# Two of four up pairs in three rounds of each MLP as units of seven products, with mixed norm operands

## The chip, the cores and the metric

The kernel runs on one core of one Trainium2 chip. The metric is the device time of one execution in microseconds, lower is better. The time before is the median of three runs, 1206.8 us (1206.55 to 1207.28 us).

## What is computed

The reference is one step of a two-layer decoder over 512 prompt tokens and 64 sample tokens that share all weights. Layer 0 mixes with retention and a gated MLP, layer 1 with sliding-window attention. Each layer ends with the part that this change touches:

```python
def sqrelu_mlp(h, w_up, w_down):
    return jnp.square(jax.nn.relu(h @ w_up)) @ w_down

hp = hp + sqrelu_mlp(rmsnorm(hp, norm_mlp[l]), mlp_w_up[l], mlp_w_down[l])
hs = hs + sqrelu_mlp(rmsnorm(hs, norm_mlp[l]), mlp_w_up[l], mlp_w_down[l])
```

The model width is 1024, the MLP width 4096, everything in float32. The 576 tokens are the columns of all activations: `h[0]` to `h[7]` hold 128 rows of the width each.

## The kernel before

TensorE (PE) multiplies in fp32r, and every operand is split into a high part and a low part. A product is three matmuls: high by high, high by low and low by high. ScalarE (ACT) casts the high part of a weight block (line 278), VectorE (DVE) subtracts it from the block to get the low part (line 289). The two parts of 128 x 512 weights are in six buffers each (`NW_`), filled ahead of use by `ahead_to`; the raw weights come by DMA, 512 KB each, into three buffers (`raw`, line 235) and a fourth one that shares its place with the tile `q` and serves every second unit of the down stage. A buffer is loaded again once `done` says that both halves of its weights are split.

An MLP runs four rounds. A round has an up stage and a down stage:

- The up stage takes eight chunks of 128 rows of the MLP's width. A chunk is 8 blocks of the width x 3 products x 2 halves of the tokens = 48 matmuls of 288 columns (line 334, `block`), with the norm's operands `xhi` and `xlo` as the moving side. DVE then applies the relu and the norm's factor to the PSUM tile `acc` (line 496), and ACT squares (line 501). Two chunks make a pair, whose four quarters are combined on DVE (`combine`, lines 533 to 536) into seven operands; these are split by ACT (`ahi`, line 504) and DVE (`alo`, line 505).
- The down stage takes four units. A unit makes a 2 x 2 block product out of seven products (the scheme of Strassen and Winograd) instead of eight: P1 to P7, each 4 blocks x 3 = 12 matmuls of 288 columns (line 346, `product`), so 84. Its weights are sums of raw blocks (s1 to s4, DVE, line 263), and its partial sums are passed on by copies in PSUM (`y`, `z`, `w`, ACT) and added to `h` by DVE (line 557). The first unit of a round runs four products over three of the four pairs first, and then over the fourth, so the last pair's operands are wanted some 36 matmuls after its start. The last unit of a round goes block by block, with the low weight part in its second matmul.

DVE and ACT keep the order in which the program is written (`manual_schedule`); PE is ordered by the scheduler. `norm.finish` (the factor `rstd`) comes after the first chunk of round 0. Below, pairs are numbered 0 to 3 and rounds 0 to 3 in each MLP.

Of the kernel before, what the change touches and what calls it, by code (L numbers as in the profile page):

```python
# [119 lines left out]
def hybrid_step(ctx: ExitStack, tc: tile.TileContext, a, o):  # L120
# [349 lines left out]
    def rounds_of(norm, nxt, mp):  # L470
        rounds, closing = 32 // FB, Closing(COL["fin"])

        def up():

            acc, got = acc_tile(), take(2)
            for k in range(KC):
                block([acc[:, hf, 0:TH] for hf in range(2)], cut(got, k), norm.xs[k], (0, 1), k == 0, k == KC - 1)
            ahead_to(used[0] + NW_ - 2)
            return acc[:, :, 0:TH]

        def flat(v):
            return v.rearrange("p a b -> p (a b)")

        for r in range(rounds):
            acts, firsts = [], []
            for p in range(FB // 2):

                q = mp.tile([P, 8, TH], F32, name="q", tag="q", bufs=1)
                hi = mp.tile([P, 7, TH], F32R, name="ahi", tag="ahi", bufs=FB // 2)
                lo = mp.tile([P, 7, TH], F32R, name="alo", tag="alo", bufs=FB // 2)  # L490
                for j in range(2):
                    view = up()
                    if r == 0 and p == 0 and j == 0:
                        norm.finish()
                    t = mp.tile([P, T], F32, name="t", tag="t")
                    nc.vector.scalar_tensor_tensor(out=halves(t), in0=view, scalar=0.0, in1=norm.rv,  # L496
                                                   op0=ALU.max, op1=ALU.mult)
# [2 lines left out]
                    seg = slice(2 * j, 2 * j + 2)  # L500
                    nc.scalar.activation(out=flat(q[:, seg]), in_=t, func=AF.Square)  # L501

                def two(s0, s1):
                    nc.scalar.copy(out=hi[:, s0 - 1:s1 - 1], in_=q[:, s0:s1])  # L504
                    nc.vector.tensor_tensor(out=lo[:, s0 - 1:s1 - 1], in0=q[:, s0:s1],  # L505
                                            in1=hi.bitcast(F32)[:, s0 - 1:s1 - 1], op=ALU.subtract)

                b12 = q[:, 0]
                combine(*(q[:, i] for i in range(8)))
                two(1, 4)  # L510
                two(4, 8)
                acts.append([[t_[:, i] for i in range(7)] for t_ in (hi, lo)])
                if nxt is None and r == rounds - 1:

                    bh, bl = (mp.tile([P, TH], F32R, name=n, tag=n, bufs=FB // 2) for n in ("b12h", "b12l"))
                    split_into(b12, bh, bl)
                    firsts.append((bh, bl))
# [884 lines left out]
def layouts(i):  # L1402
# [72 lines left out]
```

## Time and profile before

| | |
|---|---|
| runs, median of three | 1206.8 us |
| the profiled execution | 1204.73 us |
| its span, first to last instruction | 1202.9 us |
| mean granted TensorE clock | 0.997 |
| matmuls, instructions in all | 9130, 22619 |
| DMA, mean over the span | 91 GB/s, 109.43 MB |

The profile is one execution on the chip. PE is the matmuls, PEld the weight loads beside them. A row of instructions gives the start in us, the duration in us, the engine, the line, and what it writes and reads; in brackets stands how long the engine was idle before it and what ended that. The chain of waits follows from the last instruction back to what released each step. A row of the stretches view gives, for each engine, the busy time in the stretch and the instructions, then the granted clock, the DMA engines' busy share and GB/s.

### The profile page before, as it was taken

To read this page: it belongs to the slowest core of one execution; us is meant where nothing else is said; L and a number is where in the kernel's file an instruction comes from. 1 tells how busy PE (TensorE), PEld (TensorE's weight loads), DVE (VectorE), ACT (ScalarE), POOL (GpSimd) and SP (SyncE) were. 2 spreads that over 40 slices of the span, in tenths; PEclk is the share of its full clock that TensorE was granted. 3 is DMA by queue.
4 is the path that set the end of the run, shared out by engine and by line. 5 is a ranking of instruction groups with operands and counts; after the bars stand their busy time and mean duration, and the time that the engine had idled before them with its cause. 6 is when DMAs were issued, how large, how long until landed. Compare 5 with 4: busy or idle time off the path is not lost.

```text
span 1202.9 us, 22619 instructions
## 1 busy us (share of the span) xinstructions
PE 1182.9 (98%) x9130; PEld 1164.8 (97%) x9130; DVE 908.2 (76%) x1691; ACT 588.4 (49%) x1111; POOL 148.3 (12%) x130
## 2 busy tenths in 40 slices
PE   8999999999999999999999999999999999999996
PEld 8899999999999999999999998999999999999996
DVE  8977797987866876885797787546785795795696
ACT  6333554654534444443466877445453453453452
POOL 4444250000000000000002653220000000000000
PEclk9999999999999999999999999999999999999999
DMA  7343222322332232242223211122233233233322
GB/s 269 110 142 112 88 65 80 88 81 78 90 106 87 77 117 71 71 120 75 88 87 111 72 53 55 53 76 71 84 105 89 71 106 91 68 106 88 87 73 79
DMA packets 38264, 109.43 MB, mean 91 GB/s; under 512 B 4160, under 2 KB 12544, under 8 KB 38144
## 3 DMA queue, kind: packets, MB, share of 16 engines
q1 hardware_dynamic: 37440, 107.36, 29.1%
q8 instruction: 72, 1.18, 0.4%
q10 hardware_dynamic: 720, 0.62, 0.2%
q14 instruction: 32, 0.26, 0.1%
HBM read 102.92 MB, written 6.03 MB: 91 GB/s over the span
## 4 chain that ended last, share of the span: by engine, by line
PE 82%; DVE 10%; ACT 4%; DMA 3%; issue 1%; SPq 0%; DVEq 0%; ACTq 0%
PE acc L334 50%; PE acc L346 10%; PE y L346 4%; PE f L346 4%; PE w L346 3%; PE z L346 3%; DVE wlo L289 3%; DMA raw<-in_w_dn 2%; ACT s L1158 1%; DVE alo L505 1%; PE tpp L1218 1%; DVE h L557 1%; ACT ahi L504 1%; PE dn L334 1%; PE op L1233 1%
## 5 line engine op out<-in xcount | busy, mean ns | idle before, releaser
L334 PE MATMUL acc<-xhi,whi 128*128 128x288 f32 x1504 | 321.7, 295 | 0.3 <-DVE vz L809 0.3
L334 PE MATMUL acc<-xhi,wlo 128*128 128x288 f32 x1504 | 319.2, 293 | 0.0
L334 PE MATMUL acc<-xlo,whi 128*128 128x288 f32 x1504 | 318.6, 293 | 0.0
L289 DVE TENSOR_TENSOR wlo<-raw,whi 128x512 fp32r<-128x512 f32 x317 | 235.7, 757 | 68.8 <-ACT whi L278 67.5
L334 PEld LDWEIGHTS acc<-xhi,whi 128*128 128x128 f32 x1504 | 239.5, 188 | 1.6 <-issue 1.1
L334 PEld LDWEIGHTS acc<-xhi,wlo 128*128 128x128 f32 x1504 | 240.5, 188 | 0.3
L334 PEld LDWEIGHTS acc<-xlo,whi 128*128 128x128 f32 x1504 | 240.1, 188 | 0.0
L278 ACT CAST whi<-raw 128x512 fp32r<-128x512 f32 x317 | 188.9, 619 | 100.5 <-PE acc L334 73.3
L501 ACT ACTIVATE q<-t 128x576 f32<-128x576 f32 x64 | 44.0, 687 | 227.8 <-DVE t L496 227.8
L278 ACT CAST whi<-s 128x512 fp32r<-128x512 f32 x140 | 83.4, 621 | 72.4 <-DVE s L263 62.8
L496 DVE SCALAR_TENSOR_TENSOR t<-acc,rstd 128x576 f32<-128x576 f32 x64 | 48.3, 755 | 80.6 <-PE acc L334 80.4
L289 DVE TENSOR_TENSOR wlo<-s,whi 128x512 fp32r<-128x512 f32 x140 | 95.9, 697 | 10.8 <-ACT whi L278 10.8
L505 DVE TENSOR_TENSOR alo<-q,ahi 128x864 fp32r<-128x864 f32 x64 | 77.2, 1205 | 8.3 <-ACT ahi L504 8.3
L504 ACT CAST ahi<-q 128x864 fp32r<-128x864 f32 x64 | 66.6, 1041 | 13.5 <-DVE q L536 12.5
L346 PE MATMUL acc<-ahi,wlo 128*128 128x288 f32 x340 | 71.4, 298 | 0.6
L346 PE MATMUL acc<-ahi,whi 128*128 128x288 f32 x340 | 71.4, 295 | 0.0
L346 PE MATMUL acc<-alo,whi 128*128 128x288 f32 x340 | 70.4, 295 | 0.0
L1102 POOL TENSOR_TENSOR kl<-z,kh 64x512 fp32r<-64x512 f32 x4 | 5.5, 1374 | 475.1 <-ACT kh L1099 474.9
L263 DVE TENSOR_TENSOR s<-raw 128x512 f32<-128x512 f32 x70 | 48.7, 695 | 19.8 <-DMA raw<-in_w_dn 19.8
L346 PEld LDWEIGHTS acc<-ahi,wlo 128*128 128x128 f32 x340 | 53.5, 188 | 2.5 <-DVE wlo L289 2.5
L346 PEld LDWEIGHTS acc<-ahi,whi 128*128 128x128 f32 x340 | 54.0, 188 | 0.0
L346 PEld LDWEIGHTS acc<-alo,whi 128*128 128x128 f32 x340 | 53.7, 188 | 0.0
(386 smaller groups left out, 2118.8 us busy)
## 6 DMA issues: line engine op xcount, KB each, us to landing
raw<-in_w_up SPq DMA_DIRECT2D x64, 512.0 KB
raw<-in_w_dn SPq DMA_DIRECT2D x64, 512.0 KB
raw<-in_w_in SPq DMA_DIRECT2D x22, 512.0 KB
raw<-in_w_o SPq DMA_DIRECT2D x16, 512.0 KB
raw<-in_w_qkv SPq DMA_DIRECT2D x10, 512.0 KB
h<-in_xT SPq DMA_DIRECT2D x8, 288.0 KB
s<-in_s SPq DMA_DIRECT2D x4, 512.0 KB
out_ret_s<-s SPq DMA_DIRECT2D x4, 512.0 KB
```

The costliest lines, as they stand in the source:

```text
L263: nc.vector.tensor_tensor(out=sums[k, i], in0=x, in1=b[y], op=ALU.add)
L278: nc.scalar.copy(out=hi, in_=src)
L289: nc.vector.tensor_tensor(out=lo, in0=src, in1=hi.bitcast(F32), op=ALU.subtract)
L334: nc.tensor.matmul(out, lhsT=w_, rhs=x_[:, hf if isinstance(hf, slice) else half(hf)], start=(start and si == 0), stop=(stop and si == 2))
L346: nc.tensor.matmul(out, lhsT=w[wi][:, k * P:(k + 1) * P], rhs=x(k)[xi], start=(start and n == 0), stop=(stop and n == len(steps) - 1), ski ...
L496: nc.vector.scalar_tensor_tensor(out=halves(t), in0=view, scalar=0.0, in1=norm.rv, op0=ALU.max, op1=ALU.mult)
L501: nc.scalar.activation(out=flat(q[:, seg]), in_=t, func=AF.Square)
L504: nc.scalar.copy(out=hi[:, s0 - 1:s1 - 1], in_=q[:, s0:s1])
L505: nc.vector.tensor_tensor(out=lo[:, s0 - 1:s1 - 1], in0=q[:, s0:s1], in1=hi.bitcast(F32)[:, s0 - 1:s1 - 1], op=ALU.subtract)
L557: nc.vector.tensor_tensor(out=row[:, cols_], in0=row[:, cols_], in1=src, op=op)
L1158: nc.scalar.activation(out=s[:, n, cut_:], in_=s[:, n, cut_:], func=AF.Exp, bias=nm[:, n:n + 1], accum_out=den[:, n:n + 1])
L1218: nc.tensor.transpose(out=tp[:, i * P:(i + 1) * P], in_=s[:, n, hf * P:(hf + 1) * P], identity=ident)
```

## The change

In rounds 1 to 3 of each MLP, pairs 0 and 2 are no longer two chunks but one unit of seven products (`up_unit`). The activations are then the side with combinations: the norm's operands are mixed once per MLP in round 0 (`mix`, one for each two rows of `h`, after chunks 1, 2, 4 and 5), into sixteen tiles `xn`, eight of them new in the MLP's pool and eight in the place of `ks`. The weights of the unit are the same sums s1 to s4 as in a down unit, so the up weights are laid out by pairs in memory and a chunk takes the blocks of its rows in another order. The end of a pair (combining and splitting) becomes a function that runs at the start of the next pair, in a unit behind its first product. The relu and the factor are applied in a unit to quarters of 288 columns (`scaled`, min where the sign is turned), the chunk's scaling writes `q` in place of `t`, and the scratch of the DMAs that GpSimd would issue is set to 4096.

The diff, without the hunk's repetition of unchanged lines:

```diff
+MIX = ((0, 1), (1, 0), (2, 0), (2, 1))
...
+    def in_units(r, p):
+        return r > 0 and p % 2 == 0
     def mlp_order(l, last):
...
-            add_pieces([up[r * FB + f] for f in range(FB)])
+            for p in range(FB // 2):
+                pair = [up[r * FB // 2 + p, i] for i in range(2)]
+                if in_units(r, p):
+                    add_unit(pair, False)
+                else:
+                    add_pieces(pair)
...
+        operand = {"P1": 0, "P2": 2, "P3": 1, "P5": 3, "P6": 4, "P7": 5, "P4": 6}
+        mixed = []
...
-            for k in range(KC):
-                block([acc[:, hf, 0:TH] for hf in range(2)], cut(got, k), norm.xs[k], (0, 1), k == 0, k == KC - 1)
+            for n, k in enumerate((0, 1, 2, 4, 5, 6, 3, 7)):
+                block([acc[:, hf, 0:TH] for hf in range(2)], cut(got, k), norm.xs[2 * (k % 4) + k // 4], (0, 1),
+                      n == 0, n == KC - 1)
...
+        def mix(i, q):
+            a, b = 2 * i, 2 * i + 1
+            ga, gb = (cols[:, norm.gcol + c:norm.gcol + c + 1] for c in (a, b))
+            one, two_ = slice(TH, T), slice(0, TH)
+            t1, t3, u2, u4 = (q[:, n] for n in range(4, 8))
+            nc.scalar.activation(out=t3, in_=h[a][:, two_], func=AF.Copy, scale=ga)
+            for out, src, g, in1, op in ((t1, h[a][:, one], ga, t3, ALU.subtract), (t3, h[b][:, two_], gb, t3, ALU.subtract),
+                                         (u2, h[b][:, two_], gb, t1, ALU.add), (u4, h[b][:, one], gb, u2, ALU.subtract)):
+                nc.vector.scalar_tensor_tensor(out=out, in0=src, scalar=g, in1=in1, op0=ALU.mult, op1=op)
+            his, los = [], []
+            for src, sign in ((q[:, 4:6], 1.0), (q[:, 6:8], -1.0)):
+                hi, lo = (ks("xn", F32R) if i % 2 else mp.tile([P, T], F32R, name="xn", tag="xn", bufs=8) for _ in range(2))
+                nc.scalar.activation(out=halves(hi), in_=src, func=AF.Copy, scale=sign)
+                nc.vector.scalar_tensor_tensor(out=halves(lo), in0=src, scalar=sign, in1=halves(hi.bitcast(F32)),
+                                               op0=ALU.mult, op1=ALU.subtract)
...
+        def up_unit(last_pair):
+            x = acc_tile()[:, 0, 0:TH]
+            def run(n, out, start, ahead=NW_ - 1):
+                product(out, take(1)[0], lambda k: [t[operand[n]] for t in mixed[k]], range(4), start, True, True)
+                if ahead:
+                    ahead_to(used[0] + ahead)
+            def copied(name, src):
+                out = m_tile(name)[:, 0:TH]
+                nc.scalar.copy(out=out, in_=src)
+                ahead_to(used[0] + NW_ - 1)
+                return out
+            def scaled(seg, src, op):
+                nc.vector.scalar_tensor_tensor(out=q[:, seg], in0=src, scalar=0.0, in1=norm.rv[:, seg % 2],
+                                               op0=op, op1=ALU.mult)
+            run("P1", x, True, 0)
+            y = m_tile("y")[:, 0:TH]
+            nc.scalar.copy(out=y, in_=x)
+            last_pair()
+            q = q_tile()
+            ahead_to(used[0] + NW_ - 1)
+            f = m_tile("f")[:, 0:TH]
+            run("P5", f, True)
+            run("P6", x, False, 0)
+            z = copied("z", x)
+            nc.scalar.copy(out=q[:, 3], in_=f)
+            run("P2", y, False)
+            scaled(1, y, ALU.max)
+            run("P7", z, False, 0)
+            w_ = copied("w", z)
+            nc.vector.tensor_tensor(out=q[:, 2], in0=z, in1=q[:, 3], op=ALU.add)
+            scaled(2, q[:, 2], ALU.min)
+            run("P3", x, False)
+            nc.vector.tensor_tensor(out=q[:, 0], in0=x, in1=q[:, 3], op=ALU.add)
+            scaled(0, q[:, 0], ALU.max)
+            nc.scalar.activation(out=flat(q[:, 0:2]), in_=flat(q[:, 0:2]), func=AF.Square)
+            run("P4", w_, False)
+            scaled(3, w_, ALU.min)
+            nc.scalar.activation(out=flat(q[:, 2:4]), in_=flat(q[:, 2:4]), func=AF.Square)
+            return q
...
+        pending = lambda: None
         for r in range(rounds):
             acts, firsts = [], []
             for p in range(FB // 2):
-                q = mp.tile([P, 8, TH], F32, name="q", tag="q", bufs=1)
...
-                for j in range(2):
+                if in_units(r, p):
+                    q = up_unit(pending)
+                else:
+                    pending()
+                    q = q_tile()
+                for j in range(0 if in_units(r, p) else 2):
                     view = up()
...
+                    if r == 0 and (p, j) in MIX:
+                        mix(MIX.index((p, j)), q)
...
+    def up(w):
+        return w.reshape(4, 2, P, 16, 2, P).transpose(3, 4, 2, 1, 0, 5).reshape(16, 2, P, 8, P)
...
-        out[f"w_up{l}"] = chunks(i["mlp_w_up"][l])
+        out[f"w_up{l}"] = up(i["mlp_w_up"][l])
...
-    nc = bacc.Bacc("TRN2", target_bir_lowering=False, num_devices=1)
+    nc = bacc.Bacc("TRN2", target_bir_lowering=False, num_devices=1, dynamic_dma_scratch_size=4096)
```

Three places show what moves. The first is DVE in round 1 of the first MLP, around pair 2. Before, it stands between the end of pair 1 and the end of pair 2, where `t` is a scaled chunk, `wlo` a low weight part and `s1` the first sum of the coming down unit:

```order
L289 TENSOR_TENSOR wlo_4610<-raw_4409,whi_4609 128x512
L289 TENSOR_TENSOR wlo_4614<-raw_4409,whi_4613 128x512
L496 SCALAR_TENSOR_TENSOR t_4619<-acc_4560,rstd_3234 128x576
L289 TENSOR_TENSOR wlo_4672<-raw_4482,whi_4671 128x512
L263 TENSOR_TENSOR s1_4675<-raw_4617 128x512
L289 TENSOR_TENSOR wlo_4678<-raw_4482,whi_4677 128x512
L496 SCALAR_TENSOR_TENSOR t_4683<-acc_4622,rstd_3234 128x576
```

Now the same engine in the same pair, from the weights of pair 3's first chunk (`raw_4456`) to the first product of the down unit; `y`, `z`, `acc` and `w` are the unit's sums in PSUM, `raw_4663` and `raw_4700` the weights of the coming down unit:

```order
L299 TENSOR_TENSOR wlo_4680<-raw_4456,whi_4679 128x512
L299 TENSOR_TENSOR wlo_4697<-raw_4456,whi_4696 128x512
L536 SCALAR_TENSOR_TENSOR q_4637<-y_4625,rstd_3232 128x288
L299 TENSOR_TENSOR wlo_4718<-raw_4608,whi_4717 128x512
L556 TENSOR_TENSOR q_4637<-z_4677,q_4637 128x288
L536 SCALAR_TENSOR_TENSOR q_4637<-q_4637,rstd_3232 128x288
L273 TENSOR_TENSOR s1_4735<-raw_4700 128x512
L299 TENSOR_TENSOR wlo_4738<-raw_4608,whi_4737 128x512
L559 TENSOR_TENSOR q_4637<-acc_4612,q_4637 128x288
L536 SCALAR_TENSOR_TENSOR q_4637<-q_4637,rstd_3232 128x288
L273 TENSOR_TENSOR s3_4758<-raw_4700,raw_4663 128x512
L299 TENSOR_TENSOR wlo_4761<-raw_4663,whi_4760 128x512
```

Two wide scalings have become six small operations, and s1 of the down unit now stands ahead of the last weights of pair 3 and of the unit's own sums.

The second place is ACT in the same pair. Before, from the end of pair 1 on:

```order
L504 CAST ahi_4423<-q_4422 128x1152
L278 CAST whi_4609<-raw_4409 128x512
L278 CAST whi_4613<-raw_4409 128x512
L501 ACTIVATE q_4557<-t_4619 128x576
L278 CAST whi_4671<-raw_4482 128x512
```

And now, with the copies of the unit's sums, of which P7 builds on `z` and P4 on `w`:

```order
L541 COPY y_4625<-acc_4612 128x288
L603 CAST ahi_4627<-q_4491 128x864
L603 CAST ahi_4627<-q_4491 128x1152
L288 CAST whi_4638<-s3_4598 128x512
L288 CAST whi_4642<-s4_4541 128x512
L288 CAST whi_4659<-raw_4415 128x512
L531 COPY z_4677<-acc_4612 128x288
L288 CAST whi_4679<-raw_4456 128x512
L550 COPY q_4637<-f_4646 128x288
L288 CAST whi_4696<-raw_4456 128x512
L531 COPY w_4715<-z_4677 128x288
```

The copy into `z` stands behind both casts of the pair before and three casts of weights.

The third place is DVE in round 0 of the first MLP, in pair 1. Before:

```order
L289 TENSOR_TENSOR wlo_3384<-raw_3166,whi_3383 128x512
L496 SCALAR_TENSOR_TENSOR t_3389<-acc_3330,rstd_3234 128x576
L289 TENSOR_TENSOR wlo_3442<-raw_3232,whi_3441 128x512
L289 TENSOR_TENSOR wlo_3446<-raw_3232,whi_3445 128x512
L496 SCALAR_TENSOR_TENSOR t_3451<-acc_3392,rstd_3234 128x576
```

And now:

```order
L299 TENSOR_TENSOR wlo_3393<-raw_3166,whi_3392 128x512
L588 SCALAR_TENSOR_TENSOR q_3338<-acc_3339,rstd_3232 128x576
L504 SCALAR_TENSOR_TENSOR q_3338<-h2_80,cols_69,q_3338 128x288
L504 SCALAR_TENSOR_TENSOR q_3338<-h3_84,cols_69,q_3338 128x288 x3
L509 SCALAR_TENSOR_TENSOR xn_3406<-q_3338,xn_3405 128x576
L509 SCALAR_TENSOR_TENSOR xn_3410<-q_3338,xn_3409 128x576
L299 TENSOR_TENSOR wlo_3463<-raw_3230,whi_3462 128x512
L299 TENSOR_TENSOR wlo_3467<-raw_3230,whi_3466 128x512
L588 SCALAR_TENSOR_TENSOR q_3338<-acc_3413,rstd_3232 128x576
```

The six operations of a mixing stand between a chunk's scaling and the low parts of the weights of the chunk after next.

More of the change, by code (lines that the diff above doesn't have):

```diff
@@ L478, in up @@
             ahead_to(used[0] + NW_ - 2)
             return acc[:, :, 0:TH]
+        def mix(i, q):
[13 more added lines that the diff above has]
+                                               op0=ALU.mult, op1=ALU.subtract)
+                for mine, t in ((his, hi), (los, lo)):
+                    mine.extend(halves(t)[:, n] for n in range(2))
+            his, los = ([v[n] for n in (0, 2, 1, 3)] for v in (his, los))
+            parts_ = []
+            for part, mine in zip(range(2), (his, los)):
+                xa, xb = norm.xs[a][part], norm.xs[b][part]
+                parts_.append([xa[:, one], xb[:, two_], xb[:, one]] + mine)
+            mixed.append(parts_)
@@ L481, in flat, with q_tile @@
+        def q_tile():
+            return mp.tile([P, 8, TH], F32, name="q", tag="q", bufs=1)
         def flat(v):
             return v.rearrange("p a b -> p (a b)")
+        pending = lambda: None
         for r in range(rounds):
@@ L486, in rounds_of @@
             for p in range(FB // 2):
-                q = mp.tile([P, 8, TH], F32, name="q", tag="q", bufs=1)
-                hi = mp.tile([P, 7, TH], F32R, name="ahi", tag="ahi", bufs=FB // 2)
-                lo = mp.tile([P, 7, TH], F32R, name="alo", tag="alo", bufs=FB // 2)
-                for j in range(2):
+                if in_units(r, p):
[4 more added lines that the diff above has]
+                for j in range(0 if in_units(r, p) else 2):
                     view = up()
@@ L494, in rounds_of @@
                         norm.finish()
-                    t = mp.tile([P, T], F32, name="t", tag="t")
-                    nc.vector.scalar_tensor_tensor(out=halves(t), in0=view, scalar=0.0, in1=norm.rv,
+                    seg = slice(2 * j, 2 * j + 2)
+                    nc.vector.scalar_tensor_tensor(out=q[:, seg], in0=view, scalar=0.0, in1=norm.rv,
                                                    op0=ALU.max, op1=ALU.mult)
@@ L499, in rounds_of, with pending @@
                         ahead_to(used[0] + NW_ - 1)
[L500 to L517, printed above, removed]
+                    nc.scalar.activation(out=flat(q[:, seg]), in_=flat(q[:, seg]), func=AF.Square)
+                    if r == 0 and (p, j) in MIX:
+                        mix(MIX.index((p, j)), q)
+                def pending(q=q, acts=acts, firsts=firsts, r=r):
+                    hi = mp.tile([P, 7, TH], F32R, name="ahi", tag="ahi", bufs=FB // 2)
+                    lo = mp.tile([P, 7, TH], F32R, name="alo", tag="alo", bufs=FB // 2)
+                    combine(*(q[:, i] for i in range(8)))
+                    for seg in (slice(0, 3), slice(3, 7)):
+                        src = q[:, seg.start + 1:seg.stop + 1]
+                        nc.scalar.copy(out=hi[:, seg], in_=src)
+                        nc.vector.tensor_tensor(out=lo[:, seg], in0=src, in1=hi.bitcast(F32)[:, seg], op=ALU.subtract)
+                    acts.append([[t_[:, i] for i in range(7)] for t_ in (hi, lo)])
+                    if nxt is None and r == rounds - 1:
+                        bh, bl = (mp.tile([P, TH], F32R, name=n, tag=n, bufs=FB // 2) for n in ("b12h", "b12l"))
+                        split_into(q[:, 0], bh, bl)
+                        firsts.append((bh, bl))
+            pending()
+            pending = lambda: None
             between = []
```

## Prediction

> **What bounds the kernel now.** I read the page's busy shares first, then the busy time of a round's two stages, then the chain of waits, and last the rows of VectorE and ScalarE where a stage ends.
>
> ```profile
> PE 1182.9 (98%) x9130; PEld 1164.8 (97%) x9130; DVE 908.2 (76%) x1691; ACT 588.4 (49%) x1111; POOL 148.3 (12%) x130
> ```
>
> TensorE (PE) has work for 98% of the span, so time goes only where matmuls go, or where PE is made to wait. The second round of the first MLP, up stage and then down stage, in the stretches view (PE, PEld, DVE, ACT, POOL, clock, DMA):
>
> ```profile
> 349.85:399.77 49.92, 49.92 (x387) 49.92 (x385) 29.23 (x45) 19.47 (x29) 0.00 (x0) 1.00 0.27 84
> 399.77:445.05 45.28, 45.20 (x340) 44.77 (x339) 39.65 (x74) 22.90 (x42) 0.00 (x0) 1.00 0.34 96
> ```
>
> The up stage (eight chunks) never lets PE go and leaves VectorE (DVE) idle for 40%. The down stage (four units of seven products) also keeps PE busy (45.20 of 45.28) with DVE at 39.65, though it needs more DVE work for each matmul. The clock is 1.00 in both, so it drops out. The chain of waits gives the pace of each kind of matmul:
>
> ```profile
> 261.51 43.33 PE acc L334 x325
> 350.01 49.93 PE acc L334 x384
> 814.82 43.69 PE acc L334 x336
> 433.88 1.59 PE acc L346 x12
> 445.05 49.93 PE acc L334 x384
> 1093.59 49.93 PE acc L334 x384
> ```
>
> A chunk's matmul takes 49.93/384 = 130.0 ns in six up stages of like rows (the first at 350.01, the last at 1093.59) and 43.69/336 in the second MLP's first; in the first round of the first MLP it takes 43.33/325 = 133.3 ns, a slower pace for which the rows show no cause. A down unit's 84 matmuls, from 433.88 to 445.05, take 11.17 us, 133.0 ns each. A pair of chunks is 96 x 130.0 ns = 12.48 us.
>
> **The matmuls saved.** Twelve pairs (pairs 0 and 2 of rounds 1 to 3, two MLPs) become units: 12 x (96 - 84) = 144 matmuls fewer. The new units use the order of the last down unit, block by block, and that is the unit whose 11.17 us stand above. Each saves 12.48 - 11.17 = 1.31 us, in all **15.7 us**, if PE never waits longer than now. The other chunks should keep 130.0 ns: seven of the eight up stages, each right behind units, run at that.
>
> [...]
>
> **The work added on DVE and ScalarE (ACT).** Here is the end of an up pair, DVE first, then ACT:
>
> ```profile
> 387.49 0.76 DVE L496 SCALAR_TENSOR_TENSOR t<-acc,rstd 128x576 f32<-128x576 f32 x1 [1.07 <-PE acc L334]
> 388.16 0.45 DVE L533 TENSOR_TENSOR q<-q 128x288 f32<-128x288 f32 x1
> 389.00 0.46 DVE L534 SCALAR_TENSOR_TENSOR q<-q 128x288 f32<-128x288 f32 x1 [0.39 <-ACT q L501]
> 389.38 0.45 DVE L535 TENSOR_TENSOR q<-q 128x288 f32<-128x288 f32 x1
> 389.74 0.45 DVE L536 SCALAR_TENSOR_TENSOR q<-q 128x288 f32<-128x288 f32 x1
> 391.42 1.36 DVE L505 TENSOR_TENSOR alo<-q,ahi 128x1152 fp32r<-128x1152 f32 x1 [0.26 <-ACT ahi L504]
> 392.70 0.69 DVE L263 TENSOR_TENSOR s<-raw 128x512 f32<-128x512 f32 x1
> 393.30 0.69 DVE L289 TENSOR_TENSOR wlo<-raw,whi 128x512 fp32r<-128x512 f32 x1
> ```
>
> ```profile
> 388.28 0.69 ACT L501 ACTIVATE q<-t 128x576 f32<-128x576 f32 x1 [4.29 <-DVE t L496]
> 390.23 1.16 ACT L504 CAST ahi<-q 128x1152 fp32r<-128x1152 f32 x1 [0.31 <-DVE q L536]
> 382.87 1.13 ACT L278 CAST whi<-raw 128x512 fp32r<-128x512 f32 x2
> ```
>
> Starts, not durations, say what an operation costs its queue, since neighbours overlap: 0.60 us for a 512-wide sum or low part (392.70 to 393.30), 0.36 us for a 288-wide one (389.38 to 389.74), 0.67 us for the scaling of a chunk (387.49 to 388.16). A pair's whole end, scaling to second low part, is 392.70 - 387.49 = 5.21 us. ACT's casts of weights take 1.13/2, with overlap some 0.53 us.
>
> A unit needs three weight parts more than a pair (7 for 4), four sums, and four scalings with two additions at 288 wide (6 x 0.36) for two scalings at 576 (2 x 0.67). On DVE that is 7 x 0.60 + 0.8 = 5.0 us more, twice a round: 10 us in an up stage where DVE had 49.92 - 29.23 = 20.7 us free. So the sum fits. What matters is the order, for DVE and ACT work strictly in the kernel's order.
>
> **Pair 2's unit.** Behind the end of pair 1 DVE reaches the low part of P7 0.20 + 5.21 + 0.60 = 6.0 us after the unit starts; PE wants it after P1, P5, P6 and P2, 4 x 1.6 = 6.4 us. On ACT the copy that P7 builds on (z) stands behind y's copy, both casts of pair 1 and three weight casts: 390.23 + 1.16 - 387.49 + 0.20 = 4.1 us, plus 0.2 for y's copy, 3 x 0.53 and 0.4 for z, gives 6.3 us. Both come with 0.1 to 0.4 us to spare. I take 0.2 us of waiting, between 0 and 0.6 us (a pair's worth of hand-overs like 0.31 and 0.26 above), six times: **1.2 us**.
>
> **The end of pair 3.** From the end of pair 1 to the end of pair 3 PE needs 11.17 + 12.48 = 23.65 us. DVE has in between: pair 1's end 5.21; eleven low parts (three of the unit, four of pair 3, four for the next down unit) 6.6; four sums 2.4; the unit's six small operations 2.2; the unit's own end 4.54 (388.16 to 392.70) and 0.6 for the squaring before it; one scaling 0.67: 22.2 us. Add one wait: the sum s1 of the down unit needs the second of its two loads, which may start only when pair 3's first chunk is split. The rows on what a load takes and what that sum waits for today:
>
> ```profile
> 405.62 3.51 DMA raw<-in_w_dn
> 385.12 0.69 DVE L263 TENSOR_TENSOR s<-raw 128x512 f32<-128x512 f32 x1 [0.93 <-DMA raw<-in_w_dn]
> ```
>
> Between that split and s1 DVE has only a scaling, an addition, a scaling and one low part with a wait for its cast, some 1.9 us, so it waits 3.5 - 1.9 = 1.6 us (0.93 now). One low part behind a squaring on ACT adds 0.5. Together 24.3 us against 23.65: DVE comes to the last scaling 0.7 us late, with hand-overs not counted 0.9 us. Whether PE feels this is seen at today's stage end:
>
> ```profile
> 399.97 0.76 DVE L496 SCALAR_TENSOR_TENSOR t<-acc,rstd 128x576 f32<-128x576 f32 x1 [0.77 <-PE acc L334]
> 404.23 1.36 DVE L505 TENSOR_TENSOR alo<-q,ahi 128x1152 fp32r<-128x1152 f32 x1 [0.27 <-ACT ahi L504]
> 405.87 0.29 PE L346 MATMUL f<-alo,whi 128*128 128x288 f32 x1
> 409.15 0.69 DVE L263 TENSOR_TENSOR s<-raw 128x512 f32<-128x512 f32 x1 [1.43 <-DMA raw<-in_w_dn]
> ```
>
> The last low part ends at 405.59 and PE reads it at 405.87; the spare load starts then and the next sum waits for it until 409.15. There is 0.3 us of slack and then none, so I let the whole 0.9 us through, six times: **5.4 us**. Ends: 0 (the load lands a little sooner) and 2.0 us (two loads in flight share the engines), so 0 to 12 us.
>
> **The mixing in round 0.** Each of the four needs on DVE four operations at 288 and two at 576, on ACT one copy and two scalings at 576. The nearest rows are those of the norm:
>
> ```profile
> 621.99 0.84 DVE L426 SCALAR_TENSOR_TENSOR xlo<-h,cols,xhi 128x576 fp32r<-128x576 f32 x1
> 622.72 0.77 DVE L441 TENSOR_TENSOR ssq<-ssq,sq 128x576 f32<-128x576 f32 x1
> 622.47 0.77 ACT L425 ACTIVATE xhi<-h,cols 128x576 fp32r<-128x576 f32 x1
> 814.66:858.30 43.64, 43.64 (x338) 43.64 (x337) 30.81 (x48) 19.67 (x30) 0.00 (x0) 1.00 0.26 74
> ```
>
> That is 4 x 0.36 + 2 x 0.73 = 2.9 us of DVE, 11.6 us for all four, where 43.64 - 30.81 = 12.8 us are free in seven of the eight chunks. As a chain through both engines one mixing takes the squaring ahead of it 0.6, a copy 0.4, four operations 1.4, one scaling on ACT 0.7 and two low parts 1.5: 4.6 us. The tightest place is the last chunk, which needs the PSUM tile that the scaling of pair 2's second chunk frees. From the end of pair 0 to that scaling DVE's list holds two pair ends (10.4), three mixings (13.8), eight low parts and a sum (5.4) and three single scalings (2.0): 31.6 us, while PE gets there in five chunks, 5 x 6.24 = 31.2 us. So DVE is 0.4 us late there. I take 0.5 us for each round 0, between 0 and 1.5 us: **1.0 us** in all.
>
> At nothing: the chunk's scaling writes q, not t (same operation); the new order of the weight rows in memory (the loads stay 64 of 512 KB, issued in the same order); POOL and the DMA scratch (no POOL work stands in an MLP's rows).
>
> **The sum.** 15.7 - 1.2 - 5.4 - 1.0 = 8.1 us off. The profiled execution took 1204.73 us (span 1202.9 us), which gives 1196.6 us; its own median stands 2.1 us above it, at 1206.8 us, so the forecast is **1198.7 us**.
>
> **Rivals.**
> *All of it arrives.* The waits stay inside the slack: 1206.8 - 15.7 = 1191.1 us, or 1190.5 us if round 0 of the first MLP also runs at nearer 130.0 ns. For it: the down stage of the second row of the stretches view carries DVE at 39.65 of 45.28 and PE loses 0.08. Against: DVE's list for pairs 2 and 3 is longer than PE's.
> *The slower pace.* The chunks between units stay at 133.3 ns: 6 rounds x 192 x 3.3 ns = 3.8 us, 1202.5 us. For it: the row at 261.51; against: the switch to 130.0 ns behind every stage of units.
> *Slower: the load paces the round.* DVE stands at s1 with everything behind it: pair 3's weights, its scalings, the low parts that open the down stage. Each microsecond that this load lands later costs six. From (15.7 - 2.2)/6 = 2.25 us of lateness in place of 0.9, so with a landing 1.35 us later (4.9 us in place of 3.51), nothing is left. At 5.5 us it is 2.9 us a round, 17.4 us, and 1206.8 - 15.7 + 17.4 + 2.2 = 1210.7 us. For it: two loads are issued within 1.2 us of each other here. Against: the rows show 0.93 and 1.43 us of such waits today and PE hardly moved.
>
> [...]
>
> **How the numbers follow.** A measurement of this kernel can tell about 0.2% (2.4 us) from no change, so faster means below 1204.4 us and slower above 1209.2 us. The forecast, part of the saving handed back (1194 to 1204 us): 0.54. All of it: 0.17. The slower pace on top: 0.08, of which 0.07 is faster. The load or another queue paces the round: 0.13. The remaining 0.08 lies between, within 0.2%. Faster 0.78, same 0.09, slower 0.13. The range leaves out the slow rival and the very best case: 1190.5 to 1206.5 us.
>
> **What would show it.** Right: 144 matmuls fewer; the units of an up stage at 11.2 us; up stages of rounds 1 to 3 near 47.3 to 47.7 us and some 1 us of PE's idle time at the first down unit, released by DVE's low parts (alo) or the sum s1. Wrong: the chunks between units at 133 ns; PE idle inside units, released by ACT's copies; up stages of round 0 longer than 50.5 us; or waits of DVE for raw above 3 us.

## The result and the profile after

The changed kernel took 1233.5 us (median of four runs, 1233.05 to 1236.17), the kernel before 1207.0 us beside it (four runs). The ratio is 1.0227, 95% interval 1.0214 to 1.0241: it is slower by 2.3%, where the forecast was 0.7% faster. The profiled execution took 1233.05 us (span 1231.3 us).

The page's shares, as shown of before:

```profile
PE 1182.2 (96%) x8986; PEld 1156.3 (94%) x8986; DVE 996.2 (81%) x1871; ACT 635.2 (52%) x1219; POOL 148.4 (12%) x130
```

The 144 matmuls are gone (9130 to 8986), yet PE is busy as long as before: some of its time now goes to matmuls at half clock (0.50 in the first down unit of the first MLP's round 0) and at a slower pace (133.3 ns for 130.0 behind pair 2's units), and a matmul behind a wait is shown longer (0.40 us for 0.29). To see where, I cut both traces at the same places: round 0 of the first MLP, its rounds 1 to 3, and the same of the second MLP up to its last down unit. First before, then after (length, PE, PEld, DVE, ACT, POOL, clock, DMA):

```profile
261.35:349.85 88.50, 88.37 (x663) 87.90 (x662) 70.45 (x122) 42.64 (x72) 0.00 (x0) 1.00 0.30 93
349.85:635.44 285.59, 285.18 (x2163) 283.64 (x2161) 210.32 (x363) 133.00 (x223) 0.00 (x0) 1.00 0.29 87
814.66:903.55 88.89, 88.77 (x674) 88.29 (x673) 70.45 (x122) 42.58 (x72) 0.00 (x0) 1.00 0.29 85
903.55:1186.44 282.89, 282.26 (x2143) 280.95 (x2141) 202.84 (x351) 127.06 (x214) 0.80 (x1) 1.00 0.27 83
```

```profile
261.26:360.30 99.04, 92.38 (x664) 90.09 (x663) 85.77 (x150) 49.48 (x84) 0.00 (x0) 0.97 0.26 78
360.30:648.75 288.45, 280.46 (x2091) 276.98 (x2089) 239.08 (x425) 149.87 (x265) 0.00 (x0) 1.00 0.28 88
827.67:926.48 98.81, 93.21 (x674) 91.41 (x673) 85.76 (x150) 49.44 (x84) 0.00 (x0) 0.97 0.24 71
926.48:1214.95 288.47, 278.53 (x2070) 274.38 (x2069) 231.66 (x414) 144.00 (x256) 0.80 (x1) 1.00 0.26 83
```

Two losses of about the same size show. Each round 0, where only the mixing is new, is 10.5 and 9.9 us longer: 20.4 us. The rounds 1 to 3, where the units save 15.7 us, are 2.9 and 5.6 us longer instead: they gave back 15.7 + 8.4 = 24.1 us. Together 28.9 us against 28.4 us of span.

**Rounds 1 to 3.** Here are five of DVE's rows at the end of round 1's up stage, and then PE's last row of that stage and its waits in the down stage behind it:

```profile
397.39 0.69 DVE L273 TENSOR_TENSOR s<-raw 128x512 f32<-128x512 f32 x1 [2.44 <-DMA raw<-in_w_dn]
400.81 0.69 DVE L299 TENSOR_TENSOR wlo<-raw,whi 128x512 fp32r<-128x512 f32 x1 [0.66 <-ACT whi L288]
408.24 0.75 DVE L588 SCALAR_TENSOR_TENSOR q<-acc,rstd 128x576 f32<-128x576 f32 x1
410.31 1.29 DVE L299 TENSOR_TENSOR wlo<-s,whi 128x512 fp32r<-128x512 f32 x2 [1.32 <-ACT whi L288]
411.53 0.75 DVE L588 SCALAR_TENSOR_TENSOR q<-acc,rstd 128x576 f32<-128x576 f32 x1
```

```profile
407.95 0.43 PE L344 MATMUL acc<-xhi,wlo 128*128 128x288 f32 x2
409.14 0.63 PE L356 MATMUL acc<-ahi,whi 128*128 128x288 f32 x3 [0.76 <-DVE q L588]
415.57 0.40 PE L356 MATMUL acc<-alo,whi 128*128 128x288 f32 x1 [0.90 <-DVE alo L604]
423.99 0.79 PE L356 MATMUL acc<-ahi,wlo 128*128 128x288 f32 x4 [0.76 <-DVE wlo L299]
```

PE ends the last chunk at 408.38; DVE comes to its scaling at 411.53, 3.1 us late, where before it stood waiting for PE. PE pays three times: for the PSUM tile of the scaling before (0.76), for the last low part of pair 3 (0.90), for a weight's low part (0.76). The last two recur in all six rounds, the first with 0.36 to 1.57 us. The chain of waits goes through the load itself, which lands at 397.37, just ahead of the sum at 397.39:

```profile
393.06 4.31 DMA raw<-in_w_dn
```

and DVE's list of waits says how much it is over the whole kernel (us, times, longest; with before's 19.8 us, 16, 1.6 to set it against):

```profile
DVE s L273 <- DMA raw<-in_w_dn: 28.0, 14, 3.3
```

**Round 0.** The first mixing on DVE in the first MLP, between the scaling of chunk 1 and the end of pair 0, then the scaling of chunk 5; and PE's waits in the up stage and in the first down unit:

```profile
268.13 0.75 DVE L588 SCALAR_TENSOR_TENSOR q<-acc,rstd 128x576 f32<-128x576 f32 x1
270.06 2.06 DVE L504 SCALAR_TENSOR_TENSOR q<-h,cols,q 128x288 f32<-128x288 f32 x4 [1.18 <-ACT q L501]
272.03 1.60 DVE L509 SCALAR_TENSOR_TENSOR xn<-q,xn 128x576 fp32r<-128x576 f32 x2
273.54 0.45 DVE L629 TENSOR_TENSOR q<-q 128x288 f32<-128x288 f32 x1
...
299.30 0.75 DVE L588 SCALAR_TENSOR_TENSOR q<-acc,rstd 128x576 f32<-128x576 f32 x1
```

```profile
279.83 0.50 PE L344 MATMUL acc<-xhi,whi 128*128 128x288 f32 x2 [0.69 <-DVE q L588]
300.20 0.50 PE L344 MATMUL acc<-xhi,whi 128*128 128x288 f32 x2 [0.66 <-DVE q L588]
308.68 0.67 PE L356 MATMUL y<-ahi,whi 128*128 128x288 f32 x3 [1.85 <-ACT whi L288]
310.84 1.09 PE L356 MATMUL y<-ahi,wlo 128*128 128x288 f32 x3 [0.79 <-DVE wlo L299]
312.83 1.09 PE L356 MATMUL acc<-ahi,whi 128*128 128x288 f32 x3 [0.91 <-DVE q L588]
319.35 0.41 PE L356 MATMUL acc<-alo,whi 128*128 128x288 f32 x1 [0.85 <-DVE alo L604]
```

A mixing takes DVE's queue 273.54 - 270.06 = 3.48 us, four of them 13.9 us. What could take them up is the time in which DVE waited for TensorE there, in three rows of before:

```profile
279.28 0.76 DVE L496 SCALAR_TENSOR_TENSOR t<-acc,rstd 128x576 f32<-128x576 f32 x1 [1.27 <-PE acc L334]
292.08 0.76 DVE L496 SCALAR_TENSOR_TENSOR t<-acc,rstd 128x576 f32<-128x576 f32 x1 [1.37 <-PE acc L334]
304.88 0.76 DVE L496 SCALAR_TENSOR_TENSOR t<-acc,rstd 128x576 f32<-128x576 f32 x1 [1.09 <-PE acc L334]
```

That is 3.73 us (3.87 in the second MLP, counted likewise). 13.9 - 3.7 = 10.2 us and 13.9 - 3.9 = 10.0 us: the measured 10.5 and 9.9. DVE's other waits, for ACT and a load, nearly cancel: from chunk 1's scaling to chunk 5's they come to 4.9 us before and 4.6 now. Inside the up stage PE shows waits of only 1.4 us (0.69 and 0.66); the bill comes at the first down unit. There the matmuls also run at half speed (length, PE busy, clock, DMA, GB/s):

```profile
306.00:308.00 2.00, 0.82 (x7) 1.00 0.00 0
308.00:310.00 2.00, 1.32 (x6) 0.81 0.00 0
310.00:312.00 2.00, 1.13 (x4) 0.50 0.00 0
312.00:314.00 2.00, 1.17 (x5) 0.50 0.38 59
314.00:316.00 2.00, 2.00 (x10) 0.50 0.50 203
316.00:318.00 2.00, 2.00 (x17) 0.98 0.00 0
```

So the theory: **DVE's queue** loses the time, in round 0 by the mixings' length less DVE's waits for TensorE, behind pair 3 by standing at s1 for a load. The rivals: the halved clock; the lateness of round 0 carried through all rounds; units that are too much for DVE wherever they stand.

### The profile page after: what moved, and what is told of

It is laid out like the page before. It is cut to its first block, busy times and chain, and to the rows that moved or that the text cites. A ratio compares the mean times of both kernels' runs of the same rounds, so it can differ in the third digit from the quotient of the medians.

```text
span 1231.3 us, 22607 instructions
## 1 busy us (share of the span) xinstructions
PE 1182.2 (96%) x8986; PEld 1156.3 (94%) x8986; DVE 996.2 (81%) x1871; ACT 635.2 (52%) x1219; POOL 148.4 (12%) x130
## 4 chain that ended last, share of the span: by engine, by line
PE 56%; DVE 24%; ACT 10%; DMA 5%; issue 4%; SPq 0%; POOL 0%; DVEq 0%; ACTq 0%; POOLq 0%
PE acc L344 21%; PE acc L356 12%; DVE wlo L299 8%; PE f L356 4%; PE y L356 4%; DMA raw<-in_w_dn 4%; PE w L356 4%; PE z L356 4%; ACT ahi L603 2%; DVE alo L604 2%; DVE q L588 2%; DVE s L273 2%; ACT whi L288 2%; ACT q L592 1%; DVE q L504 1%
## 5 line engine op out<-in xcount | busy, mean ns | idle before, releaser
L344 PE MATMUL acc<-xhi,whi 128*128 128x288 f32 x1120 | 242.0, 297 | 2.0 <-DVE q L588 1.6
L344 PE MATMUL acc<-xhi,wlo 128*128 128x288 f32 x1120 | 239.3, 295 | 0.0
L344 PE MATMUL acc<-xlo,whi 128*128 128x288 f32 x1120 | 238.7, 295 | 0.0
L344 PEld LDWEIGHTS acc<-xhi,whi 128*128 128x128 f32 x1120 | 178.8, 188 | 4.0 <-issue 3.6
L344 PEld LDWEIGHTS acc<-xhi,wlo 128*128 128x128 f32 x1120 | 180.1, 188 | 0.3
L344 PEld LDWEIGHTS acc<-xlo,whi 128*128 128x128 f32 x1120 | 179.6, 188 | 0.0
L288 ACT CAST whi<-s 128x512 fp32r<-128x512 f32 x188 | 112.3, 619 | 86.8 <-DVE s L273 68.6
L299 DVE TENSOR_TENSOR wlo<-s,whi 128x512 fp32r<-128x512 f32 x188 | 127.0, 686 | 29.1 <-ACT whi L288 29.1
L592 ACT ACTIVATE q<-q 128x576 f32<-128x576 f32 x40 | 27.4, 686 | 91.0 <-DVE q L588 91.0
L273 DVE TENSOR_TENSOR s<-s,raw 128x512 f32<-128x512 f32 x94 | 64.4, 685 | 0.3
```

The lines of the kernel that those rows point to most:

```text
L273: nc.vector.tensor_tensor(out=sums[k, i], in0=x, in1=b[y], op=ALU.add)
L288: nc.scalar.copy(out=hi, in_=src)
L299: nc.vector.tensor_tensor(out=lo, in0=src, in1=hi.bitcast(F32), op=ALU.subtract)
L344: nc.tensor.matmul(out, lhsT=w_, rhs=x_[:, hf if isinstance(hf, slice) else half(hf)], start=(start and si == 0), stop=(stop and si == 2))
L592: nc.scalar.activation(out=flat(q[:, seg]), in_=flat(q[:, seg]), func=AF.Square)
```

## Experiments

### Which half of the change costs what

*Mixing kept, no units:* `in_units` returns False.

> The mixing is kept, no pair of up chunks is a unit (the mixed operands are made and read by nobody). Theory (the four mixings make DVE's list in round 0 longer than TensorE's work, and it is never caught up before the down stage): round 0 of each MLP costs as much as in the changed kernel, 10.5 and 9.9 us, rounds 1 to 3 cost what they did before, so 1207.0 + 20.4 = about 1227.4 us, with up to 2 us more or less. Rival (the loss of round 0 is not DVE's list but the new order of the loads and splits around it, or lies in the units): within 3 us of 1207.

Measured 1226.5 us, ratio 1.0170 (1.0153 to 1.0187). Its round 0 and rounds 1 to 3 in the first MLP:

```profile
262.76:362.00 99.24, 92.34 (x664) 89.92 (x662) 83.52 (x146) 49.50 (x84) 0.00 (x0) 0.97 0.27 83
362.00:647.33 285.33, 284.98 (x2162) 283.65 (x2161) 210.30 (x363) 132.96 (x223) 0.00 (x0) 1.00 0.28 87
```

Round 0 as long as in the changed kernel, the rest as before: the mixing alone is worth the 20 us.

*Units kept, mixing left out:*

```
-            nc.scalar.activation(out=t3, in_=h[a][:, two_], func=AF.Copy, scale=ga)
...
+            his, los = ([t[n][:, c] for t in (norm.xs[a], norm.xs[b]) for c in (one, two_)] for n in (0, 1))
```

> The units are kept, the mixing is left out: the units multiply by the norm's own operands, as many and as wide, so the output is not the reference's. Theory (rounds 1 to 3 lose by themselves what they lost in the changed kernel, 0.7 to 2.4 us each against before): 1207.0 + 8.4 = about 1215.4 us, round 0 as before. Rival (the lateness of DVE is carried over from round 0 through the rounds, and goes with the mixing): my forecast's 1198.7 plus nothing for the mixing, about 1197.7 us.

Measured 1214.6 us, 1.0074 (1.0059 to 1.0089). Round 0 and rounds 1 to 3 of the first MLP:

```profile
262.86:351.26 88.40, 88.32 (x664) 87.93 (x663) 72.73 (x126) 42.63 (x72) 0.00 (x0) 1.00 0.28 88
351.26:640.01 288.75, 280.64 (x2091) 276.73 (x2089) 238.97 (x425) 149.83 (x265) 0.00 (x0) 1.00 0.28 88
```

The rounds lose as much without the mixing (288.75 us against 288.45), so nothing is carried over from round 0. The two losses are separate.

### The mixing

*Two mixings of four:* `MIX = ((0, 1), (1, 0))`, no units.

> No units; two of the four mixings are made, behind the chunks 1 and 2 of round 0, and read by nobody. Theory (mixing costs DVE 3.48 us each, of which the waiting for TensorE in round 0, 3.73 and 3.87 us, takes its part once): 2 x 3.48 - 3.73 = 3.2 us and 3.1 us, about 1206 + 6.3 = 1212.5 us. Rival (each mixing costs its quarter of the 20.4 us of all four, by waits of its own): 1206 + 10.2 = 1216 us.

Measured 1212.1 us, 1.0057 (1.0041 to 1.0073). The two rounds 0, 92.12 and 92.48 us against 88.50 and 89.93 without mixing (the second from the run without mixing, cut alike, since its chunks also ran at 133.3 ns a matmul), are longer by 3.6 and 2.6 us; the theory said 3.2 and 3.1. Against the 88.89 us of the kernel before, at 130.0 ns, the second is 3.6 us longer. Half the mixings cost not half but about a third: the waiting for TensorE pays once.

```profile
261.33:353.45 92.12, 89.66 (x664) 88.07 (x662) 76.85 (x134) 45.99 (x78) 0.00 (x0) 1.00 0.29 90
817.66:910.14 92.48, 90.45 (x674) 89.47 (x673) 76.84 (x134) 45.97 (x78) 0.00 (x0) 1.00 0.27 82
```

*The clock held up:* matmuls of no use where PE stood idle.

```
+            def filler(k):
+                for _ in range(k if acts is fill[0] else 0):
+                    nc.tensor.matmul(fz, lhsT=ws[0][0][:, 0:P], rhs=acts[0][0][0], start=True, stop=True)
...
+                filler({"P2": 14, "P3": 6}.get(n, 0))
...
+            filler(8)
```

> The changed kernel with 28 matmuls of no use (their bank is overwritten afterwards) in front of the second, third and last of the four early groups of the first down unit, in round 0 of each MLP alone, where TensorE stood idle and its granted clock fell to 0.50. Theory (DVE's list sets the time there, TensorE waits whatever its clock): the clock stays higher and the time is the changed kernel's, 1233.5 us, within 1.5 us. Rival (the halved clock is part of the loss: 17 matmuls were started in 4.29 us where 33 go at full clock, 2.1 us a time and about as much again in the neighbouring slices): 4 to 8 us less, 1226 to 1229 us.

Measured 1235.2 us, 1.0248 (1.0232 to 1.0264). In the first MLP the clock stood at 1.00 where it had been 0.50, but it fell later, from about 319.7 to 323.1, behind two waits of 0.83 and 0.91 us; its round 0 took 99.09 us against 99.04. In the second MLP the clock stood at 1.00 through the whole round (the third row, which has the columns of all engines), and that took 98.97 us against 98.81. Nothing was won: the halved clock is an effect of the waiting, and hidden by it.

```profile
310.00:312.00 2.00, 2.00 (x17) 1.00 0.00 0
314.00:316.00 2.00, 2.00 (x17) 1.00 0.48 193
829.91:928.88 98.97, 94.75 (x702) 93.33 (x701) 85.75 (x150) 49.45 (x84) 0.00 (x0) 1.00 0.22 71
```

*The mixing on POOL:* copies on ACT, the combinations and one low part on POOL, one unit a round. (The fourth mixing stands in round 1 and reads `h`, which the down stage has changed by then, so the output isn't the reference's; the work is as long.)

```
+            for out, x, y, op in ((A1, A1, A2, ALU.subtract), (A2, B2, A2, ALU.subtract),
+                                  (B2, B2, A1, ALU.add), (B1, B2, B1, ALU.subtract)):
+                nc.gpsimd.tensor_tensor(out=out, in0=x, in1=y, op=op)
...
+            for src, eng in zip(tmp, (nc.vector, nc.gpsimd)):
+                split_into(src, hi, lo, eng)
```

> The whole computation: one unit a round (first pair; in round 1 the second pair), and the mixing's four combinations and one of its two low parts moved to POOL, which is idle there, one mixing each beside pairs 1, 2 and 3 of round 0 and pair 0 of round 1, so that DVE has one operation of 576 left in each (0.75 us, 3 us in all, where DVE waited 3.7 us for TensorE in round 0). Theory (the mixing's price was DVE's queue alone): the 7.9 us of one unit a round arrive, 1196 to 1200 us. Rival (POOL, at 0.85 us for 288 and 1.5 us for 576 wide, holds ACT, whose casts stand behind it, or slows DVE's own operations): over 1204 us.

Measured 1218.1 us, 1.0109 (1.0092 to 1.0126): the rival. Round 0 of the first MLP is 98.18 us long, 9.7 more than before, with one of a mixing's six operations left on DVE. Both halves of the rival show, in POOL's and DVE's rows:

```profile
289.94 4.11 POOL L503 TENSOR_TENSOR q<-q 128x288 f32<-128x288 f32 x4 [5.19 <-ACT q L499]
291.07 2.33 DVE L299 TENSOR_TENSOR wlo<-raw,whi 128x512 fp32r<-128x512 f32 x2 [2.08 <-ACT whi L288]
```

Beside POOL's four operations two low parts take 2.33 us, elsewhere 1.29; and DVE waits 2.08 us for a cast that stands on ACT behind the mixing's copies.

### The end of the third pair

*A fourth buffer for raw loads,* mixing left out: `bufs=4` for the tiles with tag raw, and in `load_free` `len(same) < 4 or same[-4] < done[0]`.

> Units on the first and third pair, mixing left out (the units multiply by the norm's own operands, so the output is not the reference's; this took 1214.6 us), and a fourth buffer for raw loads, so that the sum s1 of the first down unit no longer waits for a load issued late. If that wait (2.4 us of DVE in each of six rounds) is what makes DVE late behind pair 3: it goes, the PE idle time of 2.4 us in each down stage with it, about 1201 to 1203 us. Rival (DVE's list from the unit to the stage's end is too long by itself, and without the load it stands at the next thing): 1210 to 1214 us.

Measured 1193.7 us, 0.9907 (0.9893 to 0.9922), 20.9 us better than without it and more than expected. Rounds 1 to 3 of both MLPs (without the buffer 288.75 and 289.00 us, so 16.4 us are won here; DVE's waits at s1 in the six rounds fell from 15.5 to 2.0 us):

```profile
347.37:628.47 281.10, 279.43 (x2091) 276.71 (x2090) 238.88 (x425) 149.95 (x265) 0.00 (x0) 1.00 0.28 91
894.99:1175.24 280.25, 277.17 (x2071) 274.13 (x2069) 231.41 (x413) 144.06 (x256) 0.80 (x1) 1.00 0.26 83
```

The load is most of the loss, not all: these rounds are 4.5 and 2.6 us shorter than before's, 7.1 us of the 15.7 that the units save, so 8.6 us of the 25.0 that they gave back without the buffer are still lost.

*The same buffer in the kernel before,* as a control (scratch of the DMAs at 4096 there too).

> The kernel before (no units, no mixing) with a fourth buffer for raw loads, as a control. If the buffer helps where a unit stands ahead of the down stage and nowhere else but at the kernel's start (where the run with the buffer was 3.7 us ahead before the first MLP): about 1202 us. Rival (the buffer pays in every round, with or without units): under 1195 us.

Measured 1201.9 us, 0.9968 (0.9956 to 0.9980), rounds 1 to 3 as before (285.51 us in the first MLP). So 4.5 us of the buffer's gain lie outside the rounds, and the 16.4 us in the rounds are the units'.

*s1 and s3 later in DVE's list,* three buffers, mixing left out:

```
-            while summed[0] < min(len(parts) + 2, len(jobs)):
+            while summed[0] < min(len(parts) + look[0], len(jobs)):
...
             run("P2", y, False)
+            look[0] = 0 if last else 2
```

> Units on the first and third pair, mixing left out (output not the reference's), three raw buffers as in the changed kernel, but the sums s1 and s3 of the first down unit stand later in DVE's list: behind the whole end of the third pair instead of inside its unit, some 8 us later, by when their load has landed. Theory (DVE standing at s1 is what costs): as with the fourth buffer less its gain at the kernel's start, 1214.6 - 16.8 = about 1198 us. Rival (the buffer helped by letting the loads of all stages run further ahead, or the sums are now late for the weights that they make): 1208 us or more.

Measured 1202.8 us, 0.9968 (0.9956 to 0.9981). Rounds 1 to 3 of the first MLP take 282.69 us in place of 288.75, with no more memory and nothing but two sums moved. It is 5 us short of what I expected of it, and why is open; but that DVE's standing at s1 cost most of the rounds' loss is shown by both runs.

*The same in the changed kernel,* whole.

> The changed kernel, whole, with the same later place for s1 and s3. Theory (the loss of the rounds and that of the mixing add): 1233.5 - 16.8 = about 1217 us. Rival (the lateness of round 0 hides part of it): over 1222 us.

Measured 1221.0 us, 1.0130 (1.0112 to 1.0148). Round 0 99.09 us as before the move, rounds 1 to 3 of the first MLP 283.12 in place of 288.45. The losses add: the move gave 12.5 us here and some 12 without the mixing, though not the 16.8 expected of it.

### Where a unit may stand

*Only the first pair of a round,* mixing left out: `return r > 0 and p == 0`.

> As the run without mixing, but only the first pair of each of rounds 1 to 3 is a unit, the third is two chunks again (output not the reference's). Theory (what is lost is lost where a unit stands directly ahead of the last pair, whose end opens the down stage; a unit at the start of the stage has two pairs to catch up in): 6 x 1.31 = 7.9 us saved and nothing lost, about 1199 us. Rival (each unit costs DVE more than it gives TensorE, wherever it stands): half of the loss of both units, 1207 + 4.2 = about 1211 us.

Measured 1195.8 us, 0.9920 (0.9904 to 0.9937): six units do better than twelve did. It is 3 us better than expected; 1.1 us of that is round 0 of the first MLP, whose chunks ran at 130.0 ns a matmul here and at 133.3 before. No row of PE in the rounds shows a wait for DVE's scalings.

*The same with the fourth buffer.*

> Mixing left out (output not the reference's), a fourth raw buffer, and only the first pair of rounds 1 to 3 as a unit; beside the run with both units and the same buffer (1193.7 us) it tells what the third pair's unit is worth when its load no longer waits. Theory (nothing: DVE's list behind it is still longer than TensorE's, and the down stage gives back what the unit saves): within 2.5 us of it, 1191 to 1196 us. Rival (with the load out of the way it pays most of its 1.31 us, six times): 1198 us or more.

Measured 1192.3 us, 0.9891 (0.9875 to 0.9908). With the same buffer, twelve units took 1193.7: even where its load is there in time the third pair's unit earned nothing here. What it saves goes in the down stage behind it and in slower chunks (1.9 us in six rounds).

*First and second pair,* mixing left out: `return r > 0 and p < 2`.

> As many units as in the changed kernel, but on the first and second pair of rounds 1 to 3, and the mixing left out (output not the reference's). Theory (a unit makes DVE 2 to 3 us later than TensorE, a pair of chunks gives back about 1 us of waiting for TensorE; what counts is how late DVE is behind the last pair): with two pairs of chunks behind the units 0 to 1 us of lateness is left, so 1195.8 (one unit a round) - 7.9 + 0 to 6 = 1188 to 1194 us. Rival (two units a round are too much for DVE wherever they stand): as with the first and third pair, about 1214 us.

Measured 1201.6 us, 0.9979 (0.9964 to 0.9994): neither. The round's end is clean, as the theory wanted, but the second unit stands at a place the theory had not looked at, in every round:

```profile
366.55 0.40 PE L356 MATMUL acc<-xhi,whi 128*128 128x288 f32 x1 [1.04 <-ACT y L528]
```

ACT's copy y of the second unit stands behind the end of the first one. The second unit takes 12.70 us in place of 11.14 (13.03 in the last round), and in five of the six rounds the chunks behind it ran at 133.3 ns: 9.7 and 3.2 us, which accounts for 12.9 of the 13.7 us above the 1187.9 us (1195.8 - 7.9) that no lateness at all would have given.

### Versions that are whole

*One mixing in round 0, three in round 1,* units only in rounds 2 and 3, s1 and s3 late. The three add the norm's two parts first, since `h` has changed:

```
+            if i:
+                for c, n in ((a, 4), (b, 6)):
+                    nc.vector.tensor_tensor(out=flat(q[:, n:n + 2]), in0=norm.xs[c][0].bitcast(F32),
+                                            in1=norm.xs[c][1].bitcast(F32), op=ALU.add)
...
+MIX = ((0, 2, 0), (1, 0, 0), (1, 1, 0), (1, 2, 0))
...
+        return r > 1 and p % 2 == 0
```

> The whole computation: one mixing in round 0 (DVE waited 3.7 us for TensorE there, a mixing costs 3.5), three in round 1, which has no units and where DVE waited 12 us for TensorE; these three add the norm's two parts together again (two more operations of 576), 4.4 us each, since h has changed by then. Units on the first and third pair of rounds 2 and 3 alone, s1 and s3 placed late. Theory (a mixing is hidden where DVE waits for TensorE, and costs its full length where it does not): 8 units fewer than all chunks save 8 x 1.31 = 10.5 us; 0.5 to 1 us is lost in each of four rounds and 0 to 2 us in each round 1: 1200 to 1203 us. Rival (the mixing costs DVE its queue there too, up to 10 us an MLP): over 1210 us.

Measured 1203.3 us, 0.9983 (0.9973 to 0.9993). Round 0 is 88.39 us long, as without a mixing: one of 3.48 us fits into 3.73 us of waiting.

*The same with the fourth buffer* in place of the late sums.

> The whole computation, as the run with one mixing in round 0 and three in round 1, with a fourth raw buffer (the memory comes from the DMA scratch) in place of the later place of s1 and s3. Theory: the buffer alone took 4.5 us off the kernel before, and behind a unit it did better than the later place by 0.6 to 1.2 us a round, in four rounds here: 1203.3 - 4.5 - 3.6 = about 1195 us, 1194 to 1198. Rival (what the buffer saves and what the units save is the same waiting, and does not add): about 1201 us, as the kernel before with the buffer.

Measured 1198.2 us, 0.9940 (0.9928 to 0.9952): faster than both kernels, by 0.6% against before. Somewhat more than half of the 7.8 us is the buffer's, as the control shows. It is just above the range that I expected: its chunks go at the slower of two paces (133.3 ns a matmul, only the last pair's at 130.0), which the next run shows more plainly.

*And with the first pair's units alone:* `return r > 1 and p == 0`.

> The whole computation: one mixing in round 0, three in round 1, fourth raw buffer, and only the first pair of rounds 2 and 3 as a unit. Theory (a first pair's unit arrives whole, a third pair's not at all): the kernel before with the buffer took 1201.9 us; four units of 1.34 us off, 0 to 1.6 us lost behind the mixings of round 1: 1196.5 to 1198.2 us, no slower than with eight units (1198.2). Rival (the third pair's unit pays there, in rounds without other lateness): 1200 us or more.

Measured 1202.5 us, 0.9982 (0.9971 to 0.9993): the rival's number, but not for its reason. The up stage of round 2, and the same stage of the run without mixing:

```profile
443.49:493.02 49.53, 49.53 (x375) 49.53 (x373) 32.08 (x52) 22.46 (x36) 0.00 (x0) 1.00 0.30 96
```

```profile
441.37:489.95 48.58, 48.58 (x374) 48.58 (x373) 32.07 (x52) 22.46 (x36) 0.00 (x0) 1.00 0.31 97
```

PE never waits in either, the clock is 1.00 in both, DVE and ACT do the same; the six chunks go at 133.3 ns a matmul in one and 130.0 in the other. That is 0.95 us in each of four stages, 3.8 us, and 1202.5 - 3.8 = 1198.7 us is what the theory said to within 0.5 us.

## Why the prediction was wrong, point by point

**The matmuls saved: right.** 144 fewer; a first pair's unit takes 11.14 us. The chunks behind it kept 130.0 ns (12.48 us for a pair). The chunks of pair 3 did not: in all six rounds they ran at 133.3 ns, 0.3 us a round, as the rival "the slower pace" had it (these 1.9 us are part of the 8.1 below).

**Pair 2's unit: right in kind.** The six units take 11.51, 11.43, 11.23, 11.43, 11.45 and 12.51 us in place of 11.17, 2.5 us in all against 1.2; in the last, PE waits 0.86 us for the copy z.

**The end of pair 3: the mechanism was right, the size four times too small.** I had DVE 0.9 us late; in round 1 it was 3.1. Two terms make the difference. The load landed in 4.31 us, not 3.51 (it was issued at 393.06, with another one, issued at 391.85, still in flight), so the wait at s1 was 2.44 us for 1.6 (2.29 to 3.25 in the six rounds, 2.69 in the mean). And the wait for ACT's cast behind the late scaling, 1.32 us, was left out: I had counted one such wait (0.5; it took 0.66), though the longer one stands in the rows of before as well, at the same place:

```profile
397.91 1.29 DVE L289 TENSOR_TENSOR wlo<-s,whi 128x512 fp32r<-128x512 f32 x2 [1.32 <-ACT whi L278]
```

0.9 + 0.84 + 1.32 = 3.06 us. (Smaller differences nearly cancel: DVE began pair 1's end 0.5 us later than before, its other hand-overs were a little longer, and TensorE took 24.3 us for its part, not 23.65.) Pair 3's chunks, up to the down stage's first product, took 12.8 to 14.5 us for 12.48, 8.1 us in the six rounds, and the down stages behind them were 13.7 us longer: 21.8 us for 5.4. The waits at s1 alone come to 6 x 2.69 = 16.1 us, and the run with the buffer got 16.4 us back in the rounds. So for the most part it was the rival "the load paces the round", and with a load below its point of decision (4.31 us for 4.9), because the wait for the cast stood in the list as well. The rest, 8.6 us in the run with the buffer, went into slower chunks (1.9 us) and longer down stages; why these are longer is only shown in part, by PE's waits for alo and wlo.

**The mixing in round 0: the step that failed, 20.4 us for 1.0.** The list was right (chunks are numbered 0 to 7): from the scaling of chunk 1 to that of chunk 5 I counted 31.6 us, and the trace has 299.30 - 268.13 = 31.2. Two things were wrong with what I did with it. I compared it with the moment when TensorE needs the PSUM tile, which is a whole chunk later than the moment when DVE used to be there; so I saw a late start of 0.4 us (0.66 in the trace) where DVE had fallen 7.2 us behind (299.30 against 292.08). And I stopped at the last chunk of the stage. The fourth mixing comes behind that point, and the down stage, which needs DVE's last result at once, collects everything. Of the first MLP's 10.5 us, 4.1 came up to the down stage's first product and 6.4 behind it. The 12.8 us that I called free (in the second MLP) were idle time of any kind: 3.1 us of them were waits for TensorE (3.87 with the last chunk's), 8.4 were hand-overs from ACT, which stay, and 1.3 a wait for a load.

**At nothing:** the scaling into q and the new order of the rows show nowhere. **The sum:** 15.7 - 2.5 - 21.8 - 20.4 = 29.0 us slower (the spans differ by 28.4), against the forecast's 8.1 faster.

Open: why the third pair's unit pays 1.1 us a round in the whole kernel with the buffer (93.6 against 94.8 us for a round with and without it) and nothing without the mixing. The pace of the chunks covers 0.6 us of it: in the one case the unit takes the place of slow chunks, in the other the chunks behind it became slow.

## What to carry to other kernels

Here an engine's free time in a stage was not room for new work; its waits for the bounding engine were, and each could be spent once (in round 0, with 3.73 us of such waits, one mixing of 3.48 us cost nothing and two cost 3.6 us). The two PSUM tiles between TensorE and DVE hid a late engine for about one chunk (DVE was 7.2 us behind and TensorE had waited 1.4; a chunk takes 6.4 us there), so a ledger must be followed to the place where the next stage needs the last result. A wait for a load in DVE's list, which the rows show in the program's order, cost all that stood behind it (2.44 us at s1 in round 1, with the next low part's cast done at 393.89 and the low part itself at 398.00; 16.1 us in the six rounds, where the later place gave back some 12 and the buffer 16.4): move the waiting step, or give the load a buffer, before putting work in front of it.

## What the hardware showed that I had not expected

- TensorE ran the same chunks at 130.0 or at 133.3 ns a matmul, without a wait and at a granted clock of 1.00. It mostly kept to one for a whole stage (384 matmuls in 49.93 us before), but in rounds 1 to 3 of the changed kernel pair 1 ran at 130.0 and pair 3 at 133.3. Which one it was also changed between kernels that differ elsewhere (the two up stages of round 2 shown above: 133.3 and 130.0); no run shows the cause.
- The clock fell to 0.50 for some 6.8 us (309.2 to 316.1) behind a gap of 1.85 us of PE; in the filled run a gap of 1.34 us at the same place left it at 1.00, and two gaps of 0.83 and 0.91 us, 0.7 us apart, took it to 0.50 for 3.4 us. So the longest single gap alone did not tell whether it fell; no run shows what does.
- DVE's low parts went at little more than half speed beside POOL's additions and subtractions in the one row shown (two in 2.33 us, elsewhere 1.29); the rows do not show why.
